# Key transposes and scores of the samples: a bank each, or two banks in turn

## The chip, the cores and the metric

The kernel runs on one core of a Trainium2 chip. TensorE (PE) multiplies matrices and writes its products into PSUM, eight banks of 2 KB in each of 128 partitions; VectorE (DVE) and ScalarE (ACT) read the banks; GpSimd (POOL) works beside them; the DMA queue of SyncE (SP) moves data between HBM and the core's SBUF. Each engine runs its instructions in order, and semaphores make one wait for another. The metric is the device time of one execution in microseconds (us), and smaller is better.

## What is computed

One inference step of a layer with three sub-layers, over a prompt of 1024 tokens and eight samples of 16 tokens each. Each sample attends to a cache of 1024 past tokens as well. The part that matters here is the differential attention of the first sub-layer (four heads, each with two maps of 64 columns):

```python
k_all = jnp.concatenate([k_past.astype(k.dtype), k], axis=1)
v_all = jnp.concatenate([v_past.astype(v.dtype), v], axis=1)
...
s = jnp.einsum('bqhmd,bkhmd->bhmqk', q, k).astype(jnp.float32) * (HEAD_DIM ** -0.5)
s = jnp.where(mask, s + bias[None, :, None], NEG_INF)
p = jax.nn.softmax(s, axis=-1)
w = p[:, :, 0] - lam * p[:, :, 1]
return jnp.einsum('bhqk,bkhe->bqhe', w.astype(v.dtype), v)
```

Beside it the sub-layer has a causal convolution with a norm. A cross-attention to 256 memory tokens (whose keys and values the step computes for the prompt) and an MLP follow.

## The kernel before

The program has stages that follow each other: the input projections with the convolution's taps (to about 280 us of the profiled execution), the mixed stage (280 to 525 us), then the output projection, the cross-attention and the MLP, which are nearly all matmuls.

The mixed stage weaves four streams, written as Python generators in `weave` (L978): the prompt's attention (`attend`, `values`, 32 tiles of a head and 128 queries), the samples' attention, the convolution's norm, and the memory's keys and values. A scheduler then decides the order of the instructions on each engine, by priorities, by what is ready, and by which buffers are free. So a change of buffers changes the order of everything in the stage.

For one sample, `sample_keys` (L789) works through two halves c of the cached keys. A half has four groups of four transposes on PE (tile kT, L806), each into one bank; ACT copies each bank into SBUF (ku, L808). Then eight matmuls make the scores of the half (ss, L814, one bank) out of ku and the queries zq, and DVE reads that bank, adds the bias and takes the minimum (sp, L820). `sample_weights` (L825) takes the exponential on ACT (L833) and transposes the weights through the bank acc (wt, L843); `sample_values` (L847) multiplies them by the cached values (vu, L854) into the same bank (spo, L858), and the result goes out by a DMA (ds<-raw, L864). The next sample's keys are woven with this sample's values. `sample_setup` uses the tag kT too, for the transposes of the samples' own rows (t, L771).

The buffers of cached keys (kr, L548) hold four tiles of 256 tokens, which is one sample, and so do those of the cached values (vu). A load starts when the buffer is free, and SP issues the loads in the scheduled order.

The eight banks of this stage are dealt out by tags at L57 and L586, with so many for each tag:

```python
PB1 = {"sc": 2, "tr": 2, "po": 1, "kT": 1, "ss": 1, "acc": 1}
for nm, tags in (("ppsS", ("kT", "ss", "acc")), ("ppsP", ("sc", "tr", "po"))):
```

The prompt has sc (scores), tr (transposes pT, kst, qst, and those of the norm, cvt and cvT) and po (products with the values). The memory's products (mk, mv) use sc. Tiles of one tag take its banks in turn, and a tile waits until the last reader of the bank's tile before it is done.

Of the kernel before, what the change touches and what calls it, by code (L numbers as in the profile page):

```python
# [53 lines left out]
TRS = ("tr", "sc", "tr", "sc", "kT", "sx")  # L54
WP, WS, WL, WM = (0, 1), (0, 1), (.2, .8), (.2, .8)
AB = {"rq": 2, "kS": 2, "rv": 4, "qs": 2, "p": (3, 1), "wT": 2}
PB1 = {"sc": 2, "tr": 2, "po": 1, "kT": 1, "ss": 1, "acc": 1}  # L57


def f32(ap):  # L60
# [4 lines left out]
def kernel(  # L65
# [25 lines left out]
    def sm(w, tag, bufs=None):  # L91
        return small.tile([P, w], F32, name=tag, tag=tag, bufs=bufs)
# [452 lines left out]
    def load_keys(b, j):  # L545
        kr = wsk.tile([P, 2, 512], F32, name=f"kr{b}_{j}", tag="kr")
        krs[b, j] = kr
        first.append(sp.dma_start(kr, cache_k[0, b, j * 256:(j + 1) * 256].rearrange("(t p) h m d -> p t (h m d)", p=P)))  # L548
# [34 lines left out]

    p2 = ExitStack()
    ppt = {}
    for nm, tags in (("ppsS", ("kT", "ss", "acc")), ("ppsP", ("sc", "tr", "po"))):  # L586
        pl = p2.enter_context(tc.tile_pool(name=nm, bufs=1, space=PSUM, reuse_waits="tile"))
        ppt.update({t: pl for t in tags})
    ws = p2.enter_context(tc.tile_pool(name="wkS", bufs=2, side="right", reuse_waits="tile"))
# [4 lines left out]
    dcv = dram.tile([3, P, 4, 384], F32, name="dcv")  # L594
    PB = dict(PB1)

    def bk(tag, name):
        return ppt[tag].tile([P, 512], F32, name=name, tag=tag, bufs=PB[tag])
# [190 lines left out]
    def sample_keys(b):  # L789

        pm = ws.tile([P, 1152], F32, name=f"sp{b}", tag="sp", bufs=2)
        mn = [3e38]
        for c in range(2):
            sb = bk("ss", f"ss{b}_{c}")
            us = []
            for cc in range(2):
                if (b, 2 * c + cc) not in krs:
                    load_keys(b, 2 * c + cc)
                kr = krs[b, 2 * c + cc]
                u = ws.tile([P, NH, 256], F32, name=f"ku{b}_{c}_{cc}", tag="ku", bufs=UB)  # L800
                us.append(u)
                for hp in range(2):
                    ps = bk("kT", f"kT{b}_{c}_{cc}_{hp}")
                    for h in range(2):
                        for t in range(2):
                            pe.transpose(ps[:, h * 256 + t * P:h * 256 + (t + 1) * P],  # L806
                                         kr[:, t, (2 * hp + h) * P:(2 * hp + h + 1) * P], ident)
                    act.copy(u[:, 2 * hp:2 * hp + 2, :], ps.rearrange("p (h k) -> p h k", h=2))  # L808
                    yield
            with tc.high_priority(offset=TILED):  # L810

                for n, (cc, h) in enumerate([(cc, h) for cc in (1, 0) for h in (2, 3, 0, 1)]):
                    with tc.issue_after(lead) if n else ExitStack():
                        i = pe.matmul(sb[32 * h:32 * h + 32, cc * 256:cc * 256 + 256], zq[:, b, h, :], us[cc][:, h, :],  # L814
                                      start=True, stop=True)
                    lead = lead if n else i.ins
                sx["lead"] = lead
            init, mn[0] = mn[0], sm(1, "smn", bufs=8)
            add = biass if c else zero.broadcast_to([P, 512])
            dve.tensor_tensor_reduce(out=pm[:, c * 512:(c + 1) * 512], in0=sb, in1=add, scale=1.0, scalar=init,  # L820
                                     op0=ALU.add, op1=ALU.min, accum_out=mn[0])
            yield
        sx["sc", b] = (pm, mn[0])
# [43 lines left out]
    def sample_stream():  # L867
        sample_setup()
        yield from sample_keys(0)
        for b in range(8):  # L870
            yield from sample_weights(b)
            if b == 7:
                yield from sample_values(b)
                continue

            vals = sample_values(b)
            for n, _ in enumerate(sample_keys(b + 1)):
                if n % 5 == 4:
                    next(vals)
                yield  # L880
# [781 lines left out]
    for nm, an, bn, change in STEPS:  # L1662
# [3 lines left out]
        for pr in range(16):  # L1666
# [29 lines left out]
            for i in range(4):  # L1696
                c = slice(i * P, (i + 1) * P)
# [60 lines left out]
```

## Time and profile before

| | us |
|---|---|
| median of 3 runs | 1552.28 |
| lowest, highest | 1546.76, 1553.11 |
| the profiled execution | 1550.78 |
| its span, first to last instruction | 1548.9 |
| PE busy in the span | 1483.0 (96%) |
| DVE, ACT busy in the span | 1073.4 (69%), 796.3 (51%) |

The table of the whole span says that PE is what is busy, and hides that stages differ. The profile is therefore read by stretches: the mixed stage from 280 to 525 us, cut at 435 us, where the result of the fifth sample goes out, and a piece of the output projection behind it. Of each stretch one asks what PE waited for.

### The profile page before, as it was taken

Reading aid. Unit: us, or ns where it says so; the run is one execution under the profiler, and the core shown is the slowest. Engines: PE = TensorE matmul, PEld = TensorE weight load, DVE = VectorE, ACT = ScalarE, POOL = GpSimd, SP = SyncE. Lnnn points to the kernel's source line nnn. Section 1 sums busy time; section 2 is a strip of 40 time slices with the busy share of each in tenths; the row PEclk is TensorE's granted clock in tenths of the full one; section 3 lists DMA queues with packets and bytes.
Section 4 is the critical chain, followed back from the end, with each engine's and each line's share of the span. In section 5 each row is a group of like instructions: output and inputs, shape, how many; then the busy total and the mean of one; then the engine's idle time right before and its main releaser. Section 6 shows DMA issues by size and latency. Waiting matters only on the chain. (4 is left out here: it accounts for less than half of the span.)

```text
span 1548.9 us, 26040 instructions
## 1 busy us (share of the span) xinstructions
PE 1483.0 (96%) x9326; PEld 1295.8 (84%) x9326; DVE 1073.4 (69%) x2044; ACT 796.3 (51%) x1982; POOL 176.2 (11%) x327
## 2 busy tenths in 40 slices
PE   7999999788799899999999999999999999999999
PEld 6989988567687788887678999999998888878887
DVE  5899998777577664536758986667565557996564
ACT  6355272477787742635656554444353444544442
POOL 3000000122555421231010000000000000000000
PEclk9999999999999999999999999999999999999999
DMA  6423143667775833012433563454374567743443
GB/s 206 132 90 115 50 138 146 214 216 233 233 247 173 269 114 111 28 48 82 155 108 114 163 225 122 148 164 153 125 257 149 158 206 233 232 129 103 123 136 95
DMA packets 188180, 237.90 MB, mean 154 GB/s; under 512 B 23883, under 2 KB 102773, under 8 KB 188052
## 3 DMA queue, kind: packets, MB, share of 16 engines
q1 hardware_dynamic: 188052, 236.25, 47.9%
q8 instruction: 73, 1.20, 0.3%
q14 instruction: 55, 0.45, 0.1%
HBM read 172.59 MB, written 63.60 MB: 152 GB/s over the span
## 5 line engine op out<-in xcount | busy, mean ns | idle before, releaser
L124 PE MATMUL p<-Bp,Ap 128*128 128x512 f32 x448 | 174.8, 390 | 1.0 <-DVE Bp L1626 1.0
L125 PE MATMUL p<-Bp,Ap 128*128 128x512 f32 x448 | 174.2, 389 | 0.0
L123 PE MATMUL p<-Bp,Ap 128*128 128x512 f32 x448 | 157.9, 390 | 3.4 <-ACT Bp L1625 2.4
L314 DVE SCALAR_TENSOR_TENSOR acc<-cp,wc,acc 128x1024 f32<-128x1024 f32 (+2 forms) x150 | 159.3, 1071 | 1.4
L1625 ACT CAST Ap<-w_xb 128x512 fp32r<-128x512 f32 x112 | 69.4, 620 | 161.5 <-PE p L125 132.5
L1626 DVE TENSOR_TENSOR Ap<-w_xb,Ap 128x512 fp32r<-128x512 f32 x112 | 77.9, 696 | 91.4 <-ACT Ap L1625 91.4
L125 PE MATMUL p<-b_t,s 128*128 128x288 f32 x384 | 113.3, 295 | 0.0
L124 PE MATMUL p<-b_t,s 128*128 128x288 f32 x384 | 113.2, 295 | 0.0
L123 PE MATMUL p<-b_t,s 128*128 128x288 f32 x384 | 112.9, 294 | 0.0
L123 PEld LDWEIGHTS p<-Bp,Ap 128*128 128x128 f32 x448 | 83.9, 188 | 21.7 <-ACT Bp L1625 3.3
L124 PEld LDWEIGHTS p<-Bp,Ap 128*128 128x128 f32 x448 | 84.1, 188 | 20.0 <-DVE Bp L1626 2.6
L125 PEld LDWEIGHTS p<-Bp,Ap 128*128 128x128 f32 x448 | 84.1, 188 | 17.4
L124 PE MATMUL z<-wqkv,h 128*128 128x512 f32 x216 | 85.4, 396 | 0.0
L125 PE MATMUL z<-wqkv,h 128*128 128x512 f32 x216 | 85.2, 394 | 0.0
L123 PE MATMUL z<-wqkv,h 128*128 128x512 f32 x216 | 85.1, 396 | 0.0
L1454 ACT ACTIVATE o<-o 128x576 f32<-128x576 f32 x64 | 43.9, 685 | 67.3 <-DVE o L1464 29.6
L123 PE MATMUL p<-b_b,a 128*128 128x288 f32 x256 | 75.8, 296 | 0.0
L124 PE MATMUL p<-b_b,a 128*128 128x288 f32 x256 | 75.7, 296 | 0.0
L125 PE MATMUL p<-b_b,a 128*128 128x288 f32 x256 | 75.6, 296 | 0.0
L124 PEld LDWEIGHTS p<-b_t,s 128*128 128x128 f32 x384 | 72.1, 188 | 0.0
L123 PEld LDWEIGHTS p<-b_t,s 128*128 128x128 f32 x384 | 72.1, 188 | 0.0
L1090 DVE TENSOR_TENSOR XP<-pj,XP 128x512 f32<-128x512 f32 x54 | 36.9, 689 | 50.7 <-PE pj L125 50.3
(528 smaller groups left out, 4309.0 us busy)
## 6 DMA issues: line engine op xcount, KB each, us to landing
kr<-in_cache_k_dram SPq DMA_DIRECT2D x32, 512.0 KB
vu<-in_cache_v_dram SPq DMA_DIRECT2D x32, 512.0 KB
w_xb<-ds SPq DMA_DIRECT2D x64, 256.0 KB
w1t<-in_w_ff_dram SPq DMA_DIRECT2D x30, 512.0 KB
da<-o SPq DMA_DIRECT2D x48, 256.0 KB
w_xb<-da SPq DMA_DIRECT2D x48, 256.0 KB
ds<-o SPq DMA_DIRECT2D x32, 256.0 KB
dxr<-XP SPq DMA_DIRECT2D x18, 256.0 KB
```

Of the source, the lines that this page charges most:

```text
L123: pe.matmul(out, lh, rh, start=first, stop=False)
L124: pe.matmul(out, lh, rl, start=False, stop=False)
L125: pe.matmul(out, ll, rh, start=False, stop=last)
L314: dve.scalar_tensor_tensor(out=out, in0=cp[:, lo + j:hi + j], scalar=wj, in1=out, op0=ALU.mult, op1=ALU.add)
L1090: dve.tensor_add(xr[t][n], ps, xr[t][n])
L1454: act.activation(c, c, AF.Relu)
L1625: act.copy(u[:, 0], src)
L1626: dve.tensor_sub(u[:, 1], src, f32(u[:, 0]))
```

## The change

The tag ss is gone, and kT has two banks instead of one. The tile of the scores (ss in the trace) is taken from kT, and it is asked for only when the half's four groups of transposes have been written down, not before them. So the tiles of the tag follow each other as four kT, one ss, four kT, one ss, and take the two banks in turn. No instruction is added or removed. (Between L794 and the place where the tile is asked for now, line numbers are one smaller in the new file: L806 becomes L805, L808 becomes L807.)

```diff
-PB1 = {"sc": 2, "tr": 2, "po": 1, "kT": 1, "ss": 1, "acc": 1}
+PB1 = {"sc": 2, "tr": 2, "po": 1, "kT": 2, "acc": 1}
...
-    for nm, tags in (("ppsS", ("kT", "ss", "acc")), ("ppsP", ("sc", "tr", "po"))):
+    for nm, tags in (("ppsS", ("kT", "acc")), ("ppsP", ("sc", "tr", "po"))):
...
         for c in range(2):
-            sb = bk("ss", f"ss{b}_{c}")
             us = []
...
             with tc.high_priority(offset=TILED):
 
+                sb = bk("kT", f"ss{b}_{c}")
                 for n, (cc, h) in enumerate([(cc, h) for cc in (1, 0) for h in (2, 3, 0, 1)]):
```

The scheduler's order changes with it. On PE, near the start of the mixed stage, the second half of the first sample and the first half of the second one stood like this before (in kT_1_0_0 the 1 is the half, the next the pair of 256 keys in it, the last the pair of heads; wt are the first sample's weights, sc the prompt's scores):

```order
L806 MATMUL kT_1_1_0_3235<-ident,kr_3_2847 128x128 x4
L806 MATMUL kT_1_1_1_3250<-ident,kr_3_2847 128x128 x4
L814 MATMUL ss_1_3190<-ku_1_1_3234,zq 32x256 x4
L814 MATMUL ss_1_3190<-ku_1_0_3191,zq 32x256 x4
L806 MATMUL kT_0_0_0_3400<-ident,kr_0_3397 128x128 x4
L806 MATMUL kT_0_0_1_3422<-ident,kr_0_3397 128x128 x4
L843 MATMUL wt_0_3328<-ident,sp_3069 128x128 x4
L806 MATMUL kT_0_1_0_3460<-ident,kr_1_3457 128x128 x4
L701 MATMUL sc_0_0_0_3134<-kS_0_3101,qs_0_3117 128x128
```

and stand like this now:

```order
L805 MATMUL kT_1_1_0_3234<-ident,kr_3_2847 128x128 x4
L805 MATMUL kT_1_1_1_3249<-ident,kr_3_2847 128x128 x4
L814 MATMUL ss_1_3279<-ku_1_1_3233,zq 32x256 x4
L814 MATMUL ss_1_3279<-ku_1_0_3190,zq 32x256 x4
L805 MATMUL kT_0_0_0_3399<-ident,kr_0_3396 128x128 x4
L805 MATMUL kT_0_0_1_3421<-ident,kr_0_3396 128x128 x4
L805 MATMUL kT_0_1_0_3459<-ident,kr_1_3456 128x128 x4
L805 MATMUL kT_0_1_1_3485<-ident,kr_1_3456 128x128 x4
L843 MATMUL wt_0_3328<-ident,sp_3069 128x128 x4
L814 MATMUL ss_0_3495<-ku_0_1_3458,zq 32x256 x4
L814 MATMUL ss_0_3495<-ku_0_0_3398,zq 32x256 x4
```

All four transpose groups of the second sample's first half and its scores now stand ahead of the prompt's first scores, which stood among them before.

At the end of the samples' stream, also on PE, the last sample's values (spo) stood just ahead of the first products of the output projection (pj):

```order
L858 MATMUL spo_6667<-v_920,wt_6615 32x128 x4
L701 MATMUL sc_2_1_0_6257<-kS_0_5873,qs_0_5920 128x384
L702 MATMUL sc_2_1_0_6257<-kS_0_5873,ql_3090 128x384
L701 MATMUL sc_3_0_0_6286<-kS_0_5873,qs_0_5920 128x512
L702 MATMUL sc_3_0_0_6286<-kS_0_5873,ql_3090 128x512
L726 MATMUL pT_1_0_6245<-ident,p_1_0_6149 128x128 x2
L731 MATMUL po_0_6156<-vr_0_5866,wT_0_0_6159 128x128
L701 MATMUL sc_3_1_0_6333<-kS_0_5873,qs_0_5920 128x512
L702 MATMUL sc_3_1_0_6333<-kS_0_5873,ql_3090 128x512
L726 MATMUL pT_2_0_6304<-ident,p_2_0_6237 128x128 x3
L646 MATMUL kst_1_6322<-ident,r_3_1_6316 128x128 x4
L123 MATMUL pj_0_6895<-wo_4_6857,MT_6844 128x512
```

They now stand ahead of the last 37 of the memory's 96 key products (mk), of all 96 of its value products (mv), and of the preparation of the prompt's third head (kst, qst):

```order
L858 MATMUL spo_6667<-vu_6_6722,wt_6615 32x128 x8
L858 MATMUL spo_6667<-v_920,wt_6615 32x128 x4
L731 MATMUL po_6_4805<-vr_0_3767,wT_6_0_4811 128x128
L646 MATMUL kst_0_4819<-ident,r_2_0_4813 128x128
L731 MATMUL po_6_4805<-vr_0_3767,wT_6_0_4811 128x128
L646 MATMUL kst_0_4819<-ident,r_2_0_4813 128x128
L731 MATMUL po_6_4805<-vr_0_3767,wT_6_0_4811 128x128
L646 MATMUL kst_0_4819<-ident,r_2_0_4813 128x128
L731 MATMUL po_6_4805<-vr_0_3767,wT_6_0_4811 128x128
L646 MATMUL kst_0_4819<-ident,r_2_0_4813 128x128
L646 MATMUL qst_0_4907<-ident,r_2_0_4815 128x128 x4
L125 MATMUL mk_4844<-wmr_3711,mem_3707 128x256
```

Counted in rows that merge equal neighbours, the first pj stands 267 rows behind the last of these values now, and 11 rows before. Between the two orders the prompt's work ahead of the last sample has moved: 108 of its 144 products with the values stood ahead of it before, and 57 do now, as many as stood ahead of the end of the fifth sample's values before.

On DVE, at the start of the mixed stage, the reading of the score banks (the rows with ss) stands among the last convolution's taps (acc). Before:

```order
L314 SCALAR_TENSOR_TENSOR acc_2438<-cp_1793,wc,acc_2438 128x1024 x25
L820 ISA sp_3069,smn<-ss_0_3070,zero 128x512
L820 ISA smn 128x1
L314 SCALAR_TENSOR_TENSOR acc_2438<-cp_1793,wc,acc_2438 128x1024 x5
L820 ISA sp_3069,smn<-ss_1_3190,biass,smn 128x512
L820 ISA smn 128x1
```

Now:

```order
L314 SCALAR_TENSOR_TENSOR acc_2438<-cp_1793,wc,acc_2438 128x1024 x23
L820 ISA sp_3069,smn<-ss_0_3171,zero 128x512
L820 ISA smn 128x1
L314 SCALAR_TENSOR_TENSOR acc_2438<-cp_1793,wc,acc_2438 128x1024 x3
L820 ISA sp_3069,smn<-ss_1_3279,biass,smn 128x512
L820 ISA smn 128x1
L314 SCALAR_TENSOR_TENSOR acc_2438<-cp_1793,wc,acc_2438 128x1024
L830 ISA sp_3069,smn<-s_3032,biasn,smn 128x128
```

The first reading has moved ahead by two taps and the second by four in all.

## Rows read from the trace of the kernel before

**Rows 1.** The page: the span, and each engine's busy time in it.
```profile
span 1548.9 us, 26040 instructions
...
PE 1483.0 (96%) x9326; PEld 1295.8 (84%) x9326; DVE 1073.4 (69%) x2044; ACT 796.3 (51%) x1982; POOL 176.2 (11%) x327
```

**Rows 2.** Busy time in three stretches; the first line names the columns.
```profile
core 0: us, PE busy (x) PEld busy (x) DVE busy (x) ACT busy (x) POOL busy (x), PEclk, DMA share, GB/s
280.00:435.00 155.00, 124.81 (x1267) 100.60 (x1266) 103.63 (x266) 111.33 (x260) 47.72 (x86) 0.93 0.73 233
435.00:525.00 90.00, 81.93 (x801) 69.89 (x801) 62.04 (x162) 71.94 (x174) 46.54 (x69) 0.98 0.65 205
525.00:600.00 75.00, 74.39 (x387) 62.49 (x388) 44.39 (x88) 31.92 (x74) 18.92 (x29) 1.00 0.45 148
```

**Rows 3.** Timeline of SP's queue and of PE: start, us, engine, line, what.
```profile
282.58 2.03 SPq L854 DMA_DIRECT2D vu<-in_cache_v_dram  x4
...
434.08 0.89 SPq L854 DMA_DIRECT2D vu<-in_cache_v_dram  x2
435.38 0.59 SPq L864 DMA_DIRECT2D ds<-raw  x1
...
522.06 0.59 SPq L864 DMA_DIRECT2D ds<-raw  x1
...
524.95 0.50 PE L123 MATMUL pj<-wo,MT 128*128 128x512 f32 x1 [0.43 <-ACT MT L1047]
```

**Rows 4.** Waits of PE, 280 to 525 us: total us, times, longest us.
```profile
PE kT L806 <- ACT ku L808: 7.3, 12, 1.0
PE sc L701 <- ACT qs L667: 6.2, 6, 1.3
PE wt L843 <- ACT sp L833: 4.2, 5, 2.0
...
PE ss L814 <- ACT ku L808: 2.3, 4, 0.7
...
PE t L771 <- ACT zq L777: 1.5, 1, 1.5
```

**Rows 5.** Timeline of PE in the first sample; the idle time ahead in brackets.
```profile
290.29 0.66 PE L806 MATMUL kT<-ident,kr 128*128 128x128 f32 x4 [0.68 <-ACT ku L808]
291.62 0.66 PE L806 MATMUL kT<-ident,kr 128*128 128x128 f32 x4 [0.67 <-ACT ku L808]
292.95 1.07 PE L814 MATMUL ss<-ku,zq 128*32 128x256 f32 x16 [0.67 <-ACT ku L808]
```

**Rows 6.** Groups on PE, 435 to 525 us: busy us, mean ns, idle before.
```profile
L806 PE MATMUL kT<-ident,kr 128*128 128x128 f32 x64 | 10.6, 283 | 0.6 <-ACT ku L808 0.5
...
L858 PE MATMUL spo<-vu,wt 128*32 128x128 f32 x192 | 8.8, 275 | 0.0
...
L843 PE MATMUL wt<-ident,sp 128*128 128x128 f32 x27 | 4.7, 277 | 0.0
...
L858 PE MATMUL spo<-v,wt 128*32 128x128 f32 x24 | 1.6, 275 | 0.0
```

**Rows 7.** Timeline of DVE at the first sample's scores.
```profile
294.09 0.69 DVE L820 CUSTOM_DVE_ANT_0 sp<-ss,zero 128x512 f32<-128x512 f32 x1 [6.33 <-PE ss L814]
...
294.70 6.56 DVE L314 SCALAR_TENSOR_TENSOR acc<-cp,wc,acc 128x1024 f32<-128x1024 f32 x5
```

**Rows 8.** Busy time in two stretches of 20 us, columns as in rows 2.
```profile
300.00:320.00 20.00, 14.44 (x113) 10.17 (x106) 11.21 (x34) 16.23 (x38) 3.69 (x13) 0.74 0.68 215
...
460.00:480.00 20.00, 18.91 (x176) 15.51 (x174) 12.36 (x32) 16.91 (x38) 12.79 (x19) 1.00 0.94 299
```

**Rows 9.** Groups of the samples on ACT and DVE, 435 to 525 us.
```profile
L808 ACT COPY ku<-kT 128x512 f32<-128x512 f32 x16 | 9.5, 592 | 3.6 <-PE kT L806 3.6
...
L833 ACT ACTIVATE sp<-sp,smn 128x1152 f32<-128x1152 f32 x3 | 3.8, 1261 | 0.9 <-DVE smn L830 0.8
...
L820 DVE CUSTOM_DVE_ANT_0 sp<-ss,biass,smn 128x512 f32<-128x512 f32 x3 | 2.2, 746 | 0.4 <-PE ss L814 0.4
...
L844 DVE COPY wt<-wt 128x512 f32<-128x512 f32 x3 | 2.1, 691 | 2.9 <-PE wt L843 2.8
```

## Prediction

> **What bounds the kernel now.** Read first is the page's head: TensorE (PE) is busy for 96% of the span [rows 1], so time can only come out where PE stands idle or runs at the lower of its two clock levels (1.2 instead of 2.4 GHz). The table by stretches [rows 2] shows where. From 280 to 435 us PE is busy for 124.8 of 155 us, from 435 to 525 for 81.9 of 90, and from 525 on for 74.4 of 75. At 525 us the first output projection (pj) begins [rows 3], and from there PE always has a matmul that is ready. So the mixed stage, 280 to 525 us, in which the prompt's attention, the samples' attention, the memory's keys and values and the convolution's norm share the engines, has 38.3 us of idle PE, and what follows it has none worth naming. Whatever lets pj begin earlier by x us ends the program earlier by x us, since the rest is PE at work.
>
> The waits of PE in the mixed stage [rows 4] say what the idle time is. The longest is the change's own subject: the samples' key transposes (kT, four to a bank) wait 7.3 us in 12 places for ScalarE (ACT) to copy the bank out, because there is one bank. The timeline of the first sample [rows 5] shows one such turn: four transposes take 0.66 us, the copy and its signals 0.67, then the next four, and the scores wait 0.67 for the last copy too. No engine is the bound there; two of them take turns. Other waits are of the prompt (sc for qs, 6.2 us) and of the samples' softmax (wt for sp, 4.2 us).
>
> **The change, part by part.** Only the order of work and the banks change; every instruction stays, and so does the number of banks (eight).
>
> The ring itself. With two banks, four transposes can run while the last four are copied. What waited for a copy in this ring is kT 7.3 us, ss (the scores) 2.3 and t (the transposes of the samples' own rows, which use the tag kT too) 1.5 [rows 4]. Of the 7.3 us, 0.5 lies after 435 us [rows 6], so 6.8 belongs to the first stretch. The scores still need the last copy: of the 2.3 us some may stay, but the turns ahead of it are what made that copy late; I take it as gone. Sum: 10.6 us of waits.
>
> The ring's new wait. A score bank now comes out of the same two, so the second kT group behind a score group must wait until VectorE (DVE) has read that score bank (L820, 0.69 us [rows 7]), and with it all that stands behind these transposes on PE: prompt, memory, values. Where DVE is in the middle of a convolution tap it comes 1.3 us later (five taps in 6.56 us [rows 7]). In the new order eight of the fifteen such places have no cover but the first kT group and at most some five other matmuls. The cost is 0 (all covered) to 8 x (0.69 + 1.3) = 16 us; I take 0.5 us each, 4 us, because the next kT group itself (0.66 us [rows 5]) covers most of one read.
>
> The order. The scheduler now has transposes ready far more often, and puts the samples ahead: before, the last sample's values stand just ahead of pj, after all of the memory's products; now they stand ahead of 37 of its 96 key products and all its value products, with 57 of the prompt's 144 value products issued, as many as stood ahead of the *fifth* sample's end in the order before. That fifth end is the boundary at 435 us [rows 3]. So the new stage is: stretch A, up to the same point of the prompt, but with eight samples instead of five; stretch B, the rest, without samples.
>
> Stretch A. PE's work is 124.8 us [rows 2] plus three samples. Three samples' worth is in 435 to 525 us [rows 6]: values 8.8 + 1.6, weights' transposes 4.7, key transposes 10.6 (two samples of them), 25.7 us; the scores run among the values and are taken as covered by them. That gives 150.5. The clock: 300 to 320 us ran at 0.74 [rows 8], so about 10.4 us of it at 1.2 GHz, after waits like those of rows 5; at that stretch's busy share of 72% this cost some 3.7 us. I take it as gone with the waits: 146.8. Idle time: 155 - 124.8 = 30.2, less the 10.6 above, 19.6. The rest of the waits had no sample work to fill them while the bank was taken; now they have, and I take a third off (bounds: none, and all but the share that 435 to 525 us shows, 8.1 of 90): 13.1. With the ring's 4 us, A = 146.8 + 13.1 + 4 = 164 us, so it ends at 444.
>
> Stretch B. What stood from 435 to 525 us without three samples: PE 81.9 - 25.7 = 56; ACT at most 71.9 - 9.5 - 3.8 = 58.6; DVE at most 62.0 - 2.2 - 2.1 = 57.7 [rows 2, 9]. Three engines with about the same load, in the chain of the prompt's softmax, and no filler: it cannot be far below 56, and would be 90 if the samples had only filled holes. With all streams, stretch 280 to 435 had PE busy for 80%; I take 56 / 0.78 = 72 us. So pj begins at 444 + 72 = 516 instead of 525.
>
> **The sum:** 9 us less. The profiled execution took 1550.78 us around its span of 1548.9; the median of the three runs is 1552.28, 1.5 above it. Forecast: 1552.3 - 9 = 1543.3, say 1543 us. Within 0.5% (7.8 us) is about what a measurement of this kernel can't tell from no change.
>
> **Rivals.** *Transfers become the bound (slower).* Up to 435 us 233 GB/s x 155 us = 36.1 MB moved [rows 2]; 48 cache loads of 512 KB (24 of keys, 24 of values, issued from 282.6 to 434.1 us [rows 3]) are 25.2 of it and 10.9 is other. In A there are 60 such loads: 42.4 MB. At the best 20 us that the mixed stage shows, 299 GB/s at a share of 0.94 [rows 8], this is 142 us and fits; at the mean of today, 233, it is 182 us: A ends at 462, pj at 534, and the kernel takes 1561 us. It decides below 42.4 MB / 173 us = 245 GB/s. For it: the key buffers hold one sample, so loads start only as transposes free them. Against: no row of PE's waits names a transfer, and at 299 GB/s PE was busy for 18.9 of 20 us [rows 8]. The Trainium skill (Perfetto Trace Analysis, Roofline) gives a core's sixteen DMA engines about 435 GB/s together; by that figure A would need an estimated 97 us for its transfers and this rival would fall away. The row with 299 GB/s at a share of 0.94 speaks for a lower ceiling here, and the rival stays. [...]
>
> *The tail gives it back (no change).* The samples were the filler of the last 90 us. Without them B is a prompt chain with PE, ACT and DVE all at 56 to 59 us, and takes 80 us instead of 72; pj begins at 524, and the time is 1551. For it: in 435 to 525 us most of PE's own waits are already for prompt work. Against: memory products and the norm's transposes are still there as filler.
>
> *A larger gain.* A's idle falls to about 6 us with the ring covered (153 us), B to 66: pj at 499, the time 1526. For it: 435 to 525 us runs at 91% busy.
>
> *The ring's new wait is dear.* All 16 us of it: A 176, pj at 528, the time 1555.
>
> **How the numbers follow.** Forecast with its neighbours (gain of 3 to 16 us) 0.46; tail 0.22; transfers 0.14; larger gain 0.12; ring 0.06. Faster by over 0.5%: six tenths of the first (0.28), the larger gain (0.12) and 0.02 of the tail, 0.42. Slower: transfers 0.13, tail 0.04, ring 0.03, together 0.20. Within 0.5%: 0.38. The range reaches from near the larger gain to the transfers' price: 1529 to 1561; the forecast's own is 1536 to 1549.
>
> **What would show it.** Right: the kT rows of the first sample without 0.67 us of idle; waits of PE for ku near 1 us in all; the last output of the samples (ds<-raw) near 445 us instead of 522; pj at 513 to 520. The transfers: 42 MB by that point at 280 GB/s or less, with waits that name kr or vu. The tail: idle PE over 20 us between the last sample and pj, released by DVE p or ACT qs. The ring: waits of kT for DVE sp. I am wrong at the root if pj moves and the end does not, since then the last 1024 us were not PE's work alone.

## The result and the profile after

The changed kernel takes 1559.3 us (median of 7 runs) beside 1551.06 of the kernel before; the ratio is 1.0062, 95% interval [1.0045, 1.0078]. It is slower by 8 us, where 9 us less was forecast. The profiled execution took 1556.67 us, the shortest of the seven. The page's head hardly shows the loss: over the whole span PE is as busy as before [rows 1]. (Of the 12 instructions more in its first line none is counted as work of an engine; the numbers behind the x are those of before.)

```profile
span 1554.8 us, 26052 instructions
...
PE 1482.1 (95%) x9326; PEld 1292.1 (83%) x9326; DVE 1070.7 (69%) x2044; ACT 797.7 (51%) x1982; POOL 173.3 (11%) x327
```

Busy time of the three stretches of [rows 2], columns as there:

```profile
280.00:435.00 155.00, 133.00 (x1528) 105.58 (x1529) 101.78 (x275) 120.38 (x281) 42.42 (x81) 0.99 0.83 278
435.00:525.00 90.00, 67.97 (x509) 58.33 (x508) 54.44 (x137) 58.89 (x141) 44.40 (x70) 0.91 0.52 169
525.00:600.00 75.00, 72.85 (x381) 60.27 (x380) 46.89 (x97) 33.27 (x80) 21.91 (x35) 1.00 0.28 85
```

Up to 435 us all is better than before: PE is busy for 8 us more, at a clock of 0.99 instead of 0.93, and 278 GB/s move instead of 233. From there to 525 us PE is busy for 68 us instead of 82, and even behind 525 us it idles for 2.2 us instead of 0.6. The two marks of [rows 3], from the samples' last output on SP's queue and the first product of the output projection on PE (the times at the end are of the first and last of the group):

```profile
L864 SPq DMA_DIRECT2D ds<-raw x8: 589/590/667, 311.1 to 444.8; - x8
```
```profile
L123 PE MATMUL pj<-wo,MT x72: 390/393/498, 525.3 to 593.6; 128*128 128x512 f32 x72
```

The last sample ends at 444.8 us, 77 us earlier than before. The projection begins at 525.3, no earlier than before. (The two profiled executions are not level at the start of the stage: its first transpose of the prompt starts at 277.5 us here and at 280.3 before, behind code whose order is the same up to there. So the stage itself has become 3 us longer, 247.8 us instead of 244.7.)

Waits of PE up to the end of the samples, 277 to 445 us, which answer to [rows 4]:

```profile
PE ss L814 <- ACT ku L807: 3.1, 6, 0.7
...
PE kT L805 <- DMA kr<-in_cache_k_dram: 2.4, 3, 1.3
...
PE kT L805 <- ACT ku L807: 2.2, 5, 0.7
...
PE kT L805 <- DVE smn L820: 0.5, 2, 0.3
```

and of the part without samples, 445 to 526 us:

```profile
PE sc L701 <- ACT qs L667: 5.4, 2, 4.0
PE pT L726 <- ACT zt L631: 5.1, 2, 4.9
PE pT L726 <- DVE p L715: 2.4, 3, 1.5
PE qst L646 <- issue: 1.8, 1, 1.8
```

Of the waits that the change was about, kT for ku is 2.2 us instead of 7.3, ss for ku 3.1 instead of 2.3, and the ring's new wait (kT for VectorE's smn) is 0.5. What stops PE now is the prompt, in few long pieces. The two longest are seen in ACT's timeline:

```profile
462.52 0.62 ACT L113 CAST wmr<-wmv_0r 128x512 fp32r<-128x512 f32 x1 [1.08 <-DMA wmv_0r<-in_w_mv_dram]
...
465.66 0.67 ACT L631 ACTIVATE zt<-cvT,hln 128x384 f32<-128x384 f32 x1 [1.16 <-DMA dcv<-zt]
...
482.35 0.62 ACT L113 CAST wmr<-wmv_1r 128x512 fp32r<-128x512 f32 x1 [1.47 <-DMA wmv_1r<-in_w_mv_dram]
...
483.26 0.67 ACT L666 ACTIVATE qs<-qst,gqk 64x512 fp32r<-64x512 f32 x1
```

Each time ACT stands in front of a transfer (a cast of the memory's weights, or the store that frees zt), and the copy that PE needs is queued behind it. From 461.5 us PE, which works in order, stood for 4.9 us at a transpose (pT) that wanted the bank zt was read from. This raised three theories: the samples' lead leaves the prompt alone at the end (lead theory); the memory's casts and products are what is wrong there (memory theory); the loads of the residual (XP, eighteen of 256 KB), which take the samples' buffers and so follow the last sample at once (447.4 us here, 522.8 before), make the loads and stores late (burst theory). The rival to all three is that sharing the banks costs something itself.

### The profile page after: what moved, and what is told of

Its sections match the earlier page's. It is cut to its first block, busy times and chain, and to the rows that moved or that the text cites. A ratio compares the mean times of both kernels' runs of the same rounds, so it can differ in the third digit from the quotient of the medians.

```text
span 1554.8 us, 26052 instructions
## 1 busy us (share of the span) xinstructions
PE 1482.1 (95%) x9326; PEld 1292.1 (83%) x9326; DVE 1070.7 (69%) x2044; ACT 797.7 (51%) x1982; POOL 173.3 (11%) x327
## 4 chain that ended last, share of the span: by engine, by line
PE 44%; DVE 3%; DMA 2%; issue 1%; ACT 0%; SPq 0%; DVEq 0%; ACTq 0%
PE p L124 13%; PE p L125 13%; PE p L123 13%; PE pj L124 1%; PE pj L123 1%; PE pj L125 1%; DMA w_xb<-ds 1%; DVE Ap L1626 1%; PE hft L1389 1%; PE smp_p L125 0%; PE smp_p L124 0%; PE smp_p L123 0%; DVE Bp L1626 0%; DVE w_HC L1676 0%; DMA wmo_3r<-in_w_mo_dram 0%
## 5 line engine op out<-in xcount | busy, mean ns | idle before, releaser
L1454 ACT ACTIVATE o<-o 128x576 f32<-128x576 f32 x64 | 43.9, 686 | 72.6 <-DVE o L1464 29.8
L124 PEld LDWEIGHTS p<-b_t,s 128*128 128x128 f32 x384 | 72.1, 188 | 0.0
L123 PEld LDWEIGHTS p<-b_t,s 128*128 128x128 f32 x384 | 72.0, 188 | 0.0
L125 PEld LDWEIGHTS p<-b_t,s 128*128 128x128 f32 x384 | 71.9, 188 | 0.0
```

What stands on the lines that cost most here:

```text
L123: pe.matmul(out, lh, rh, start=first, stop=False)
L124: pe.matmul(out, lh, rl, start=False, stop=False)
L125: pe.matmul(out, ll, rh, start=False, stop=last)
L1454: act.activation(c, c, AF.Relu)
```

## Experiments

All times are medians, each beside the kernel before as measured with it (1549.4 to 1552.0 us). The intervals of e1 and e5 overlap with that of the changed kernel, so a difference of 3 us from it is hardly clear of noise.

| run | banks | what else is different | us | ratio, 95% |
|---|---|---|---|---|
| changed kernel | shared | | 1559.3 | 1.0062 [1.0045, 1.0078] |
| e9 | shared | order of before | 1546.2 | 0.9970 [0.9952, 0.9988] |
| e10 | own | order of the changed kernel | 1585.9 | 1.0231 [1.0202, 1.0260] |
| e15 | shared | one sample | 1525.5 | 0.9843 [0.9807, 0.9879] |
| e1 | shared | samples curbed | 1556.6 | 1.0035 [1.0022, 1.0048] |
| e2 | own | samples raised | 1556.5 | 1.0036 [1.0023, 1.0049] |
| e3 | shared | memory early | 1551.6 | 1.0007 [0.9994, 1.0019] |
| e4 | shared | memory late | 1569.0 | 1.0116 [1.0099, 1.0132] |
| e6 | own | memory early | 1559.6 | 1.0060 [1.0041, 1.0079] |
| e7 | own | memory late | 1580.5 | 1.0188 [1.0167, 1.0208] |
| e5 | shared | XP held, order drawn up anew | 1556.1 | 1.0044 [1.0029, 1.0059] |
| e11 | shared | XP moved in one piece, rest as changed | 1573.0 | 1.0143 [1.0117, 1.0170] |
| e13 | shared | XP moved in three, rest as changed | 1573.8 | 1.0147 [1.0130, 1.0164] |
| e8 | shared | memory early, XP held | 1556.6 | 1.0041 [1.0025, 1.0058] |
| e12 | shared | samples curbed, XP held | 1550.6 | 0.9996 [0.9981, 1.0011] |
| e14 | shared | as e12, memory earlier | 1562.8 | 1.0075 [1.0060, 1.0090] |

### The banks alone, and the order alone

Both programs trace the same instructions on each engine in the same sequence; only the scheduler then orders them differently. So one kernel can be held to the other's order. ORDER lists all traced instructions in the order in which the other kernel issues them, and each is tied to the one ahead of it on its engine (an edge of issue order, without a semaphore):

```diff
+    tr = nc.cur_bb.bb.instructions
+    last = {}
+    for n in array.array("H", zlib.decompress(base64.b85decode(ORDER))):
+        i = tr[n]
+        if i.engine in last:
+            tc.add_manual_dep(i, last[i.engine].name, ...NoSync..., reason="order")
+        last[i.engine] = i
```

> The change of banks alone: transposes and scores share two banks as in the changed kernel, but every engine and SP's queue is held to the order of the kernel before, instruction by instruction. Gain theory (what the prediction took for the banks themselves): waits of TensorE for ku fall from 9.6 us to 3 or less, nothing else moves, 1543 to 1548. Cost theory (a score bank that VectorE has not read holds the next transposes, and all behind them): 1553 to 1559, with waits of kT for VectorE's smn of several us. If what is saved on one engine is waited for on another: 1551 within 2 us.

Measured: 1546.2 us, 5 us less than before, as the gain theory had it, though the waits for ku fall to 4.6 us and not to 3. Of the kernels here that do the whole work it is the fastest.

> The change of order alone: a bank for the transposes and one for the scores as before, but every engine and SP's queue is held to the order of the changed kernel, instruction by instruction. Order theory (the loss is the order's, and the banks themselves help): at least the changed kernel's loss, and the waits for copies on top of it, 1560 to 1568, with 10 us or more of TensorE's waits for ku. Bank theory (the loss is that of sharing): 1551 within 2 us.

Measured: 1585.9 us, worse than either theory said. Its longest wait of PE, 277 to 555 us:

```profile
PE kT L806 <- ACT ku L808: 30.2, 34, 3.2
```

So the loss is the order's, and the banks help: by 5 us in the old order (1551.1 to 1546.2), by 27 in the new one (1585.9 to 1559.3), which has its transposes closer together. The order alone costs 13 us with shared banks (1546.2 to 1559.3) and 35 with own ones (1551.1 to 1585.9). No kernel was held to its own order, so what the ties themselves cost is not measured; it seems little, since behind the last sample e10 takes 82 and 97 us (below), and the changed kernel, without ties, 80 and 97. The same two orders side by side, busy time from the start of the stage to the first pj and from there to the last omT (a transpose of the attention's result for the projection's second half), a mark with the same work ahead of it in both (2537 and 2536 instructions of PE in these windows); first e9, then the changed kernel:

```profile
279.00:519.00 240.00, 202.14 (x2069) 169.17 (x2068) 165.95 (x427) 183.46 (x433) 93.51 (x155) 0.96 0.69 229
519.00:610.00 91.00, 89.72 (x468) 74.92 (x466) 53.30 (x106) 37.46 (x85) 22.80 (x33) 1.00 0.45 148
```
```profile
277.00:525.00 248.00, 203.41 (x2054) 165.94 (x2053) 159.12 (x414) 180.74 (x422) 88.39 (x150) 0.96 0.71 236
525.00:622.00 97.00, 93.05 (x482) 76.63 (x482) 58.46 (x120) 41.34 (x95) 25.83 (x39) 1.00 0.33 102
```

PE's idle time is 37.9 + 1.3 = 39 us in the old order and 44.6 + 4.0 = 49 in the new, and the work itself takes 4.6 us more (296.5 against 291.9). The second row has 14 instructions more in the new order: some of the prompt is left over behind pj. By place, PE idles in the changed kernel for 25.0 us up to the last sample (277 to 445 us) and for 19.6 from there to pj; in e9 it is 28.8 up to 435 us and 9.1 from there:

```profile
277.00:445.00 168.00, 142.96 (x1656) 113.83 (x1655) 111.72 (x293) 126.03 (x292) 45.94 (x86) 0.99 0.79 261
```
```profile
279.00:435.00 156.00, 127.25 (x1313) 104.97 (x1312) 107.90 (x277) 115.22 (x268) 47.37 (x86) 0.95 0.73 239
435.00:519.00 84.00, 74.88 (x759) 64.20 (x758) 58.05 (x151) 68.24 (x166) 46.14 (x69) 1.00 0.63 209
```

And the end of the new order does not care about banks. Here is e10, up to its last sample, to pj and to the last omT, and under it the changed kernel from its last sample to pj:

```profile
277.00:472.00 195.00, 152.88 (x1641) 119.92 (x1643) 111.38 (x291) 128.40 (x291) 45.71 (x86) 0.94 0.67 225
472.00:554.00 82.00, 62.97 (x420) 54.31 (x413) 48.38 (x124) 55.13 (x131) 42.14 (x64) 0.88 0.54 178
554.00:651.00 97.00, 94.31 (x483) 78.14 (x483) 59.15 (x120) 41.78 (x96) 25.52 (x39) 0.98 0.33 102
```
```profile
445.00:525.00 80.00, 60.45 (x401) 52.11 (x400) 47.39 (x122) 54.72 (x130) 42.45 (x64) 0.89 0.56 183
```

With own banks the part with samples takes 195 us instead of 168, and the part without them 82 against 80.

### The prompt's chain by itself

```diff
+ONE = 1
...
+        if b == ONE - 1:
+            for x in range(ONE, 8):
+                sp.dma_start(ds[:, x], raw)
...
-        for b in range(8):
+        for b in range(ONE):
             yield from sample_weights(b)
-            if b == 7:
+            if b == ONE - 1:
```

> The changed kernel with the attention of seven of the eight samples left out: only the first sample's keys, weights and values are worked through, and its result is written for all eight, so the samples' outputs are not the reference's. It measures the pace of the rest (prompt, memory, norm) when next to no sample work is there to fill TensorE. TensorE's work from the stage's start to the first output projection is 192 us with eight samples; one sample's is about 13 us (64 transposes of 0.12, 16 score matmuls of 0.1, 36 of the values of 0.07, 9 of the weights of 0.12), so about 101 us are left with one. If TensorE is the bound and idles for a fifth, as in the prediction's 0.78: 129 us from the start of the stage to the first output projection, 119 less than the changed kernel. If the prompt's own chain sets the pace of a stretch without samples (its last part took 81 us for 51 of the 108 value products ahead of the first output projection): 108 products take 171 us, 77 less than the changed kernel, and TensorE is busy for 60% of them.

Measured: 1525.5 us, and 216 us from the start of the stage to pj, far over both numbers expected (129 and 171). The 13 us for a sample were too many: a sample has 32 transposes, and 64 are those of two [rows 6]. Counted in the traces, once where they overlap, the samples' products and transposes (kT, ss, spo, wt) keep PE busy for 94 us in the kernel before, 85 in the changed kernel and 15 here. So 79 us of PE's work are gone against the kernel before, and 24 us of time; against the changed kernel it is 70 and 34. Busy time from the start of the stage to the first pj, and to the last omT:

```profile
278.00:494.00 216.00, 159.49 (x1034) 128.17 (x1033) 140.30 (x351) 138.27 (x328) 89.51 (x150) 0.81 0.42 135
494.00:593.00 99.00, 95.42 (x490) 78.75 (x488) 60.39 (x122) 41.91 (x99) 26.34 (x39) 0.98 0.32 100
```

216 us for the prompt, the memory and the norm, with PE busy for 159, DVE for 140 and ACT for 138, so no engine's load is the bound: the prompt's steps follow each other from engine to engine, in the order that the scheduler drew up for this kernel. The pace is 2.0 us for each of 108 value products, slower than the 1.6 us of the changed kernel's last part (100 instructions, two for each product, in 80 us). Part of this is the clock, granted at 0.81 to a PE that often stands: the same lack of other work that leaves it idle makes its work slower. For the bound it is enough that seven samples, 79 us of matmuls, cost 24 us in the kernel before. They ran mostly in gaps of the prompt, and an order that runs them ahead of it leaves later gaps empty.

(The Trainium skill, Perfetto Trace Analysis, Optimization Strategies, says that where the matmul engine waits for others, those that block the critical path are to be made faster. Here that path is a chain over three engines that are all busy for 74% or less of the time, so no single one of them is the one to speed up.)

### The samples' lead

```diff
-PRI = (300, -50, 0, -100, 100, 50)
+PRI = (300, -50, -200, -100, 100, 50)
```

> The changed kernel with the samples' priority at -200 instead of 0, so that the prompt goes ahead of them. In its order on TensorE 72 of the prompt's 144 value products stand ahead of the last sample's values, instead of 57 in the changed kernel and 108 in the kernel before; the banks are those of the changed kernel. Lead theory (the samples run ahead and leave the prompt's last part without other work to fill TensorE): the loss falls with those 51 products, 8.2 x (108 - 72) / 51 = 5.8 us, so about 1557, 2 to 3 us below the changed kernel; idle TensorE between the last sample and the first output projection below 15 us, from 19.7. Bank theory (transposes and scores in the same two banks wait for each other): the banks are as in the changed kernel, so the loss stays at 8 us, 1559, within 1 us.

Measured: 1556.6 us, the lead theory's number; PE is busy for 41.0 of 53 us from the last sample to pj, 12 us idle.

For e2 the kernel before has +400 there.

> The kernel before, each with its own bank, and the samples' priority at +400 instead of 0. In its order 78 of the prompt's 144 value products stand ahead of the last sample's values, instead of 108. Lead theory: slower than the kernel before by 8.2 x (108 - 78) / 51 = 4.8 us, about 1556, with 10 us or more of idle TensorE between the last sample and the first output projection (1.8 before). Bank theory: the banks are those of the kernel before, so the time is that of the kernel before within 2 us, about 1551.

Measured: 1556.5 us, again the lead theory's number; 8.6 of 39 us are idle at the end, a little less than expected. So with own banks throughout, an order with a longer lead of the samples is some 5 us slower. These two orders differ from their neighbours in other places too, so this is support, not proof.

### The memory's place

```diff
-WP, WS, WL, WM = (0, 1), (0, 1), (.2, .8), (.2, .8)
+WP, WS, WL, WM = (0, 1), (0, 1), (.2, .8), (0, .4)
```

> The changed kernel with the memory's stream at the beginning of the mixed stage (0 to 0.4 instead of 0.2 to 0.8 of it). All 192 memory products and all casts of their weights now stand ahead of the last samples; behind the last sample only the prompt and the rest of the norm are left, with 73 of 144 value products ahead of it. Lead theory (what the end lacks is other work for TensorE): the end loses 133 products, some 17 us of filler, so the idle time between the last sample and the first output projection stays at 18 us or more although there are fewer prompt products behind, and the time is no better than the changed kernel: 1559 to 1563. Load theory (the end is long because ScalarE stands in the casts of the memory's weights, which wait for late loads, with the prompt's copies behind them): those casts are gone from the end, and with them some 4 to 5 us of waits of TensorE for zt and qs: 1554 to 1556.

> The changed kernel with the memory's stream at the end of the mixed stage (0.5 to 1 instead of 0.2 to 0.8). All 192 memory products stand behind the last sample now (133 in the changed kernel), with 64 of the prompt's 144 value products ahead of it instead of 57. Lead theory: 59 products more, some 8 us of filler, at the end and 7 prompt products fewer: faster than the changed kernel by 3 to 6 us, 1553 to 1556. Load theory: all sixteen casts of the memory's weights, and their loads, fall into the end, where ScalarE's copies for the prompt stand behind them: slower than the changed kernel by 2 to 5 us, 1561 to 1564.

Measured: 1551.6 (e3) and 1569.0 us (e4, which has (.5, 1) in the place of (0, .4)). Both go against the lead theory's reading that any matmul at the end is welcome. They go the load theory's way (it is the memory theory by another name), but 2 and 5 us beyond its ranges, so it has the sign and not the size: the memory's products fill PE, but each group of them waits for casts and loads, and these stand in ACT's and SP's order. The same with own banks:

> The kernel before, each with its own bank, with the memory's stream at the beginning of the stage (0 to 0.4), as the run with shared banks and early memory had it, which took 1551.6 us. Memory theory (what the changed order loses is the memory's products, casts and loads in the prompt's last part, whatever the banks): no memory products stood behind the last sample before, and none do now, so nothing to lose or gain: 1551 within 2 us. Bank-gain theory (the shared banks do save the 7 us that transposes wait for copies, and the place of the memory hid it): with own banks these waits stay, so this kernel is slower than the one with shared banks by 5 to 7 us: 1557 to 1559.

> The kernel before, each with its own bank, with the memory's stream late (0.5 to 1). In its order 144 of the 192 memory products stand behind the last sample's values, with 87 of the prompt's 144 value products ahead of it; in the changed kernel it is 133 products and 57. Memory theory: a loss like the changed kernel's or larger, without any change of banks: 1558 to 1564. Bank theory (sharing two banks is what costs): none of it here, 1551 within 2 us. Lead theory (filler at the end helps): no loss, or a gain.

Measured: 1559.6 and 1580.5 us. Early is no gain here but a loss of 8 us, near the bank-gain theory's 1557 to 1559; late loses 29, far more than any theory said. Put together, own against shared banks: 1559.6 to 1551.6 with the memory early, 1551.1 to 1559.3 at its place in both kernels, 1580.5 to 1569.0 with the memory late. Sharing gains 8 and 11.5 us in two of the three places and loses 8 in the third. So the sign of the change's result hangs on the place of another stream.

### The loads of the residual

e5 holds them behind the last store of the memory's values, and the scheduler draws up a new order:

```diff
...
-            sp.dma_start(xr[t][n], xf[t][:, n * 512:(n + 1) * 512])
+            with tc.issue_after(sx["hold"]):
+                sp.dma_start(xr[t][n], xf[t][:, n * 512:(n + 1) * 512])
```

> The changed kernel with the eighteen loads of the residual (XP, 256 KB each, wanted by the output projection) queued behind the last store of the memory's values. In the changed kernel they follow the last sample's result at once, from 447.4 us on, since they take the samples' buffers, and stand in SP's queue ahead of the memory's weight loads and the norm's stores. Burst theory (these transfers make wmv_0r, and the store that zt waits for, late): TensorE's wait of 4.88 us for zt and ScalarE's of 1.08 for wmv_0r at 462 us go, the first output projection begins at 519 to 521 instead of 525, and the time is 1553 to 1555. Lead theory (the end is long because the prompt is alone there): another of its waits takes the place, 1558 to 1560.

Measured: 1556.1 us, 3 less than the changed kernel and between the two expectations. That leaned to the burst theory, but here everything else may have moved too. e11 and e13 hold every engine to the changed kernel's order and move these loads alone on SP's queue.

> The changed kernel, with PE, ACT, DVE and POOL held to its order; on SP's queue only the eighteen loads of the residual (XP) are moved, behind the last store of the memory's values. The run that held these loads before let the scheduler draw up the rest anew, and took 1556.1 us; here nothing else moves. Burst theory: TensorE's 4.88 us for zt and ScalarE's 1.08 for wmv_0r at 462 us shrink, 1553 to 1556. If the end of the stage is the prompt's own chain: 1558 to 1560.

Measured: 1573.0 us, outside both expectations. Moved in one piece they made the next load, wo_5r, late. ACT's wait for it, 480 to 560 us:

```profile
ACT wo L113 <- DMA wo_5r<-in_w_out_dram: 14.1, 2, 13.2
```

> The changed kernel, every engine held to its order, and on SP's queue the eighteen loads of the residual (XP) moved behind the loads of the convolution's results (zc), six behind each group of four, much as they stand in the kernel before; the run that put all eighteen in one piece ahead of wo_5r made that load 12 us late, with ScalarE's cast and TensorE behind it, and took 1573 us. Here wo_5r keeps its place. Burst theory (of the loss of the order, part is that these 4.7 MB stand ahead of the memory's weights and the norm's stores at 447 to 467 us): TensorE's 4.88 us for zt shrink to 1 or less, the first output projection begins by 521, 1554 to 1556. If the prompt's chain takes that time anyway: 1558 to 1560.

Measured: 1573.8 us, again outside both. PE's waits, 440 to 640 us:

```profile
PE pj L123 <- DVE XP L1090: 10.9, 2, 5.6
PE sc L701 <- ACT qs L667: 5.0, 3, 3.4
PE pT L726 <- ACT zt L631: 3.6, 3, 3.2
```

The wait for zt shrinks only from 4.9 to 3.2 us and the one for qs from 4.0 to 3.4; pj begins at 525.5, where it began before the loads were moved, and then waits 10.9 us for XP. The burst theory falls: moving the loads saves about 2 us in these two waits and nothing in pj's place, and they are wanted where they stand. What e5 gained, if it did, came from the order that was drawn up around them. With the memory early, holding them loses 5 us:

> Shared banks with the memory's stream early (that kernel took 1551.6 us) and the residual's loads held behind the result of the prompt's third head, fifth tile, so that neither casts of the memory's weights nor that burst of loads meets the prompt's last part. If the burst costs something there too: 1547 to 1550. If what is left is the prompt's own chain (14 us of idle TensorE behind the first output projection, waits for p, MT and o): 1551 to 1552.

Measured: 1556.6 us, outside both expectations.

### Remedies together

> Shared banks, the samples' priority at -200 (1556.6 us alone) and the residual's loads behind the last store of the memory's values (1556.1 us alone). If they take away different parts of the loss of 8.2 us, the sum is 1559.3 - 2.7 - 3.2 = 1553.4, so 1552 to 1555. If both take away the same part: 1556 to 1557.

Measured: 1550.6 us, better than the sum, level with the kernel before.

> Shared banks, samples at -200, the residual's loads held behind the memory's last store (1550.6 us so far), and the memory's stream from 0.1 to 0.7 of the stage instead of 0.2 to 0.8. 48 of the memory's 192 products stand behind the last sample's values, instead of 77. Memory theory (casts of the memory's weights in the prompt's last part are the rest of the loss): 1545 to 1548. If what is left is the prompt's own chain: 1550 within 2 us.

Measured: 1562.8 us, outside both expectations and 12 us worse than e12. The memory theory falls as a rule for all orders: there pj begins at 511.6 us, but from there to the last omT 10.2 of 114 us are idle (PE busy for 103.8), with prompt work left over. Each new order moves the total by several us in a direction that no single theory told.

**What is settled and what is not.** Settled for these two orders, since nothing else was changed: the banks gain, and the order loses more. Where it loses is behind the last sample: 80 us for 50 value products there, and 97 us from pj to the last omT; in the old order with the same banks (e9) 83 us, from 435 to 518 us, hold 48 value products and the last samples as well, and 91 us follow. Shown too: the stage without seven samples takes 216 us with no engine busy for more than 74% of it, so there the chain of steps limits it and not the load of an engine. Not settled is what makes one order better than another at the end, and how the 13 us divide between the memory's casts, single waits and leftover prompt work. An earlier load of the second set of memory weights in the changed order wasn't tried: their raw buffers are of a ring (tag r) that the memory's own outputs take too.

## Why the prediction was wrong

**The ring: right in direction, its size halved.** 10.6 us of waits were to go. In e9, where nothing else moves, kT for ku falls from 7.3 to 2.3 us, while ss for ku stays at 2.3 [rows 4]. The turns of the first sample have not gone either: in the changed kernel eight transposes run in one piece where four did, and then PE waits for ACT's copies as before [rows 5]; the waits for ku, which were to be near 1 us in all, are 5.3 in the changed kernel:

```profile
288.06 1.09 PE L805 MATMUL kT<-ident,kr 128*128 128x128 f32 x8 [0.68 <-ACT ku L807]
289.39 0.66 PE L805 MATMUL kT<-ident,kr 128*128 128x128 f32 x4 [0.24 <-ACT ku L807]
290.72 1.07 PE L814 MATMUL ss<-ku,zq 128*32 128x256 f32 x16 [0.68 <-ACT ku L807]
```

Waits of PE in e9, the whole stage:

```profile
PE wt L843 <- ACT sp L833: 5.9, 5, 2.4
PE po L731 <- ACT o L742: 3.8, 4, 1.7
...
PE ss L814 <- ACT ku L807: 2.3, 4, 0.7
PE kT L805 <- ACT ku L807: 2.3, 4, 0.7
```

The wait for sp was 4.2 us [rows 4] and the one for o 2.3, so 3.2 of the 5.0 us that kT saves are waited for in these two places, and PE's idle time as a whole hardly falls: 38.3 us before (245 less 206.7 busy), 37.9 in e9. The 5 us come from the work, 202.1 us instead of 206.7: the clock is 0.96 instead of 0.95, and the 256 transposes alone take 41.0 us instead of 42.9. (The ends of matmuls are modelled in a profile, so how a gain divides between idle and busy time is rough.) (The Trainium skill, Perfetto Trace Analysis, Optimizing Tensor Performance, advises rotating independent groups through different banks so that copies overlap with matmuls; e9 agrees, with 5 us.)

**The ring's new wait: too dear by far.** 4 us were taken, with 16 as the bound; 0.5 was measured.

**Stretch A: nearly right, in part by luck.** 164 us were forecast; the last output goes out 167 us after the start of the stage, at 444.8 us on the clock of the trace (forecast 444). But PE's work took 143.0 us instead of 146.8, and its idle time was 25.0 instead of the 17.1 that were made up of 13.1 and the ring's 4: two errors that partly cancel.

**Transfers: no bound, as forecast.** From 277 to 445 us 261 GB/s moved, 43.9 MB (42.4 were reckoned). The sign that was named for this rival was there to the letter (280 GB/s or less, and waits for kr), but these waits are 2.4 of 25.0 us. Nor was 299 GB/s the most that the queues move; shortly behind the last sample it was 392:

```profile
455.00:461.00 6.00, 4.49 (x31) 3.61 (x31) 4.95 (x17) 2.87 (x10) 2.20 (x6) 1.00 1.05 392
```

**Stretch B: the step that failed.** It was taken as 56 us of PE's work at the mean utilisation of a stretch that had all the streams, 72 us. It took 80, 19.6 of them idle and at a granted clock of 0.89. The text had the three engines' loads (56 to 59 us) right for PE and ACT, which took 60 and 55, and too high for DVE (47), and the rival "tail" had 80 us to the microsecond, but as a case of 0.22. What it should have been sized by is the pace of the prompt: 52 value products between 435 and 525 us before, with three samples beside them; 50 in 80 us without. Taking 25.7 us of sample work away shortened that stretch by 10. Nor is it the banks: e10 takes 82 us there. A mean utilisation belongs to the mix of streams it was read in, and does not carry over to one of them alone.

**"What follows pj is PE at work": the second step that failed.** From pj on PE had next to no idle time before, and the text took that as a property of the place. But the prompt goes on behind pj, and more of it was left there: from pj to the last omT it is 97 us instead of 91, with 4.0 us idle where e9 has 1.3. The work left over is small (13 matmuls and transposes of 477), and the idle time is mostly pj's own (waits of PE, 525 to 622 us):

```profile
PE pj L123 <- ACT HC L133: 1.9, 1, 1.9
PE pj L123 <- DVE XP L1090: 1.1, 1, 1.1
```

The text had named this sign itself: pj's place did not tell the end. The plainest case is e3, where pj begins at 482.3 us, 43 us earlier than before, and the time is that of the kernel before (1551.6 us):

```profile
L123 PE MATMUL pj<-wo,MT x72: 390/394/505, 482.3 to 581.7; 128*128 128x512 f32 x72
```

Behind the last omT nothing moved: 933 us in both. Added up, A with 167 us for 164, B with 80 for 72 and 97 for 91 behind pj make the 17 us between the 9 less that were forecast and the 8 more that were measured.

**The rival on the slow side was the wrong one.** Transfers got 0.14, at 1561 us; the time landed beside that number by another way. "Tail" had the place and the size of the lost time in B, but its price stopped at pj (1551). And 0.5% (7.8 us) was taken as what a measurement can't tell from no change; a change of 8 us came out clear of it, with bounds of 7 and 12 us.

## What to carry over

Where a scheduler draws up the order, a change of buffers is two changes. Hold one kernel to the other's order, and measure them apart: here the one meant was worth 5 us, and the one that came along cost 13. Before filler work is moved ahead of a chain, ask at what pace the chain runs when it is alone (leave the filler out and measure): if it is slow there, the filler is free only beside it.

## What the runs showed of the hardware

The clock was low behind a gap. After 4.9 us without a matmul, at 466 us of the changed kernel, the memory's products start every 0.21 us, and 4 us later every 0.12. The granted clock, the last column but two, was 0.50 first and 1.00 then (PE's timeline, and busy time as above):

```profile
470.18 0.41 PE L123 MATMUL mv<-wmr,mem 128*128 128x256 f32 x1
470.39 0.41 PE L124 MATMUL mv<-wmr,mem 128*128 128x256 f32 x1
...
474.13 0.28 PE L124 MATMUL mv<-wmr,mem 128*128 128x256 f32 x1
474.25 0.28 PE L125 MATMUL mv<-wmr,mem 128*128 128x256 f32 x1
```
```profile
468.00:471.00 3.00, 3.00 (x16) 3.00 (x15) 1.54 (x5) 3.00 (x10) 1.94 (x4) 0.50 0.59 203
472.00:476.00 4.00, 4.00 (x36) 4.00 (x35) 0.56 (x1) 1.30 (x4) 3.35 (x5) 1.00 0.05 15
```

So this gap was paid for twice. In e15, with gaps throughout, the granted clock of the stage is 0.81, and taking 79 us of work away gave back only 24 us against the kernel before (70 and 34 against the changed one). Not expected either was how much order alone is worth: with the same instructions, e9 and e10 lie 40 us apart, and the memory's place alone moved the kernel with its own banks by 29.
